# Attention over all heads as one sequence, and TensorE in source order from the first value unit on

## The chip, the cores and the metric

The kernel runs on one core of one Trainium2 chip. The metric is device microseconds (us) of one execution. The time of the kernel before is the median of three runs; a profile comes from one further execution, recorded by the hardware profiler.

## The reference, cut to what matters

One block of a hybrid model, sequence 512, width 2048, float32 throughout: a norm, one large input projection `w_in`, a state-space mixer (SSD) and an attention mixer side by side, the output projection `w_out`, and a gated feed-forward part.

```python
u = rmsnorm(h, attn_norm_w)
z, xbc, dt_raw, q, kc, vc, ks, vs, kw, vw, gate_raw = split(u @ w_in)
y_ssd = ssd_mixer(z, xbc, dt_raw, ...)        # ends: rmsnorm(y * silu(z), norm_w)
y_att = nsa_mixer(q, kc, vc, ks, vs, kw, vw, gate_raw, ...)
h = h + concatenate([y_ssd, y_att]) @ w_out
v = rmsnorm(h, ffn_norm_w)
h = h + (silu(v @ w_gate) * (v @ w_up)) @ w_down
out = rmsnorm(h, final_norm_w)

# nsa_mixer: 16 query heads of 64 in 4 groups; each group shares one key/value head
k_cmp = silu(flat(kc + pe_k) @ w1_k) @ w2_k   # 31 blocks of 32 tokens; v_cmp alike
o_cmp = softmax(q . k_cmp, masked) @ v_cmp
o_sel = softmax(q_rot . rope(ks) over the chosen blocks) @ vs    # 8 of 8 blocks
o_win = softmax(q_rot . rope(kw), window 512) @ vw
y_att = g0*o_cmp + g1*o_sel + g2*o_win        # g = sigmoid(gate_raw)
```

With 512 tokens the choice takes all 8 blocks and the window spans the sequence, so `o_sel` and `o_win` are both full causal attention, each with its own keys and values. They are the two branches (`br` 0 and 1) below.

## The kernel before, in words

**Units.** Both projections are cut into units of 128 output columns: 41 input units (`w_in`), then 16 output units (`w_out`). `run_unit` loops over the contraction in steps of 128. The activations stand in SBUF as `u`, a high and a low part; weights arrive as `wraw` (256 KB loads on SyncE's (SP's) queue, a ring of four) and are split into `whi` (ScalarE, ACT) and `wlo` (VectorE, DVE). A step `k` issues three matmuls into a bank `ps_g`, and after them the scheduler of the source, `Sched`, ticks once:

```python
pe.matmul(p, hi_t[i][:, j, :], ah, start=(k == 0), stop=False)                  # L234
pe.matmul(p, hi_t[i][:, j, :], al, start=False, stop=False)                     # L235
pe.matmul(p, lo_t[i][:, j, :], ah, start=False, stop=(k == u.nk - 1))           # L236
sch.tick()
```

An input unit has 16 steps; the output units have 11, 11, thirteen times 12, and 8 (table `NS`), and the rest of `w_out` is added by the part behind them.

**Tasks.** Everything else is a generator task: `yield n` means that the task goes on n ticks later, and a task can wait for flags that others set. So the source interleaves the tasks' instructions with the units' matmuls; how closely is set by the yields. `run_until(flags)` ticks on the spot, without any unit matmul between, until the flags are there.

**Two orders.** The framework has a scheduler of its own that moves instructions on every engine against source order. Only within `tc.manual_schedule(engines=PE)` does TensorE (PE) keep the order of the source. Before the change that holds from the first output unit on (`units[NU:]`, NU = 41).

**Order of the input units.** Gates and time steps, the state-space inputs, the four that feed the compression, `z` tiles 0 to 3, then for each group g its remaining `z` tiles (g=1: two, g=2: one, g=3: one), values `VS`, keys `KS` and two query units `Q`. A z tile's evacuation multiplies `silu(z)` with the mixer's row tile, stores the product to DRAM (`gy`) and adds its square to `acc2` (square on ACT, sum on POOL); after tile 7 `rms_stats` makes the second norm's row `row2`.

**Compression.** `compress()` (L599 to L681) takes 16 blocks of `w1` weights, eight for keys, then eight for values. A block: a load `w1r` (GpSimd (POOL) queue, two buffers), its split into `w1h` (ACT) and `w1l` (DVE), the inputs `xh` and `xl`, then six matmuls into `ps_s` (L630 to L632). Then two tails, for keys and values: transposes (L642), `hf`, `hh`, `hl`, small matmuls with `w2` (L663 to L665 and L677 to L679), and out come `kch`, `kcl` and `vcmp`. `pre_att`, run ahead of the first value unit, calls `run_until("cmp", ...)`, so that in the source the whole compression ends ahead of that unit's matmuls.

**Attention.** It loops over the four groups. At a group's start it waits for the group's keys, values and both query units, then does the compressed softmax (`sc`), its transposes `cph`, `cpl`, and four pairs of copies into `vpad`. Then come 32 items (head, branch, block of 128 queries): a score (two matmuls with `kh`, `kl` and the rotated queries `rq` into a bank `ps_s`, L834 and L835; DVE's mask-and-minimum L838 empties the bank into `e`; ACT's exponential), three items later the transposes (L863 into `ps_t`, split into `pth` and `ptl`), and after four transposed items the value matmuls (L873, L874, L879 into `ps_v`). An item takes 1 tick plus `PACE[s % 4]` ticks, or `PACE_OUT` once the output units have begun. A query unit's evacuation makes the rotated queries (rope: four small DMAs `sw` on POOL's queue, POOL arithmetic), `uq` on POOL, and the compressed scores (L776, L777 into `ps_m`, 16 pairs of small matmuls a unit).

**The end of the input units.** `pre_ms`, ahead of the last input unit, starts `ms_in`: eight times a `gy` row tile is loaded, multiplied by `row2` on POOL (L134), and written, scaled, over the first half of `u` (high part ACT, low part DVE L972). `ma_in` does the same for attention rows that went to DRAM. The first output unit reads both.

**PSUM.** Besides two banks `ps_g` the tasks share `ps_s`, `ps_t`, `ps_m` and `ps_v`.

Of the kernel before, what the change touches and what calls it, by code (L numbers as in the profile page):

```python
# [29 lines left out]
PACE = [2,2,2,3]  # L30
PACE_OUT = [1,2,1,2]
LAG = 3
# [83 lines left out]
def body(ctx, tc, xT, w_in, w_out, w_gate, w_up, w_down, w1k, w1v, cols, rows, kst, out):  # L116
# [35 lines left out]
    def ps_t():  # L152
        return ps("t", 2)
# [394 lines left out]
    def ev_z(t):  # L548
        def ev(p):
# [209 lines left out]
    def ev_q(g, j):  # L759
        def ev(p):  # L760
# [6 lines left out]
            yield 2  # L767
# [19 lines left out]
    def attention():  # L787
# [6 lines left out]
        for g in range(4):  # L794
            yield from sch.wait(("k", g), ("v", g), ("q", g, 0), ("q", g, 1))
            kh, kl = R["k", g]
            v = R["v", g]

            sc = R["sc", g]
            sm = ap.tile([128, 3, 4, 4], F32, tag="sm", name="sm", bufs=1)  # L800
            dve.tensor_reduce(sm[:, 0], sc, AX.X, ALU.max)
            dve.tensor_scalar(sm[:, 0], sm[:, 0], -1e20, None, op0=ALU.max)
            dve.tensor_tensor(sc.rearrange("p i h k -> p (i h) k"), sc.rearrange("p i h k -> p (i h) k"),
                              sm[:, 0].rearrange("p i h -> p (i h)")[:, :, None].to_broadcast([128, 16, 32]),
                              ALU.subtract)
            act.activation(sc, sc, AF.Exp, scale=0.125)
            for h in range(4):
                a_hi(vpad[32 * h:32 * h + 32, h, 0:64], vcmp[:, g, :])
                lo(dve, vpad[32 * h:32 * h + 32, h, 64:128], vcmp[:, g, :], vpad[32 * h:32 * h + 32, h, 0:64])
# [4 lines left out]
            mul(dve, sc.rearrange("p i h k -> p (i h) k"), sc.rearrange("p i h k -> p (i h) k"),  # L814
                sm[:, 2].rearrange("p i h -> p (i h)")[:, :, None].to_broadcast([128, 16, 32]))
            yield 6
            p = ps_t()
# [7 lines left out]
            yield 2  # L825

            items = [(h, br, i) for h in range(4) for br in range(2) for i in range(4)]
            pt, pr, po = {}, {}, {}

            def score(h, br, i):  # L830
                L = 128 * (i + 1)
                q = R["rq", g, h // 2][:, h % 2, i * 128:(i + 1) * 128]
                p = ps_s()
                pe.matmul(p[:, 0:L], q, kh[:, br, 0:L], start=True, stop=False)  # L834
                pe.matmul(p[:, 0:L], q, kl[:, br, 0:L], start=False, stop=True)  # L835
                e = ap.tile([128, 512], F32, tag="e", name="e", bufs=EB)
                m = ap.tile([128, 4], F32, tag="em", name="em", bufs=EB + 1)
                dve.tensor_tensor_reduce(e[:, 0:L], p[:, 0:L], kcs(K_AM + 512 - L, L), -0.125, 3e38,  # L838
                                         ALU.add, ALU.min, m[:, 0:1])
                act.activation(e[:, 0:L], e[:, 0:L], AF.Exp, scale=-1.0, bias=m[:, 0:1], accum_out=m[:, 1:2])  # L840
                pr[h, br, i] = (e, m)

            def norm(h, br, i):
                L = 128 * (i + 1)
                e, m = pr[h, br, i]
                gc = (4 * g + h) * 3 + 1 + br
                dve.reciprocal(m[:, 2:3], m[:, 1:2])
                if br:
                    dve.tensor_scalar(e[:, 0:L], e[:, 0:L], m[:, 2:3], gat[:, i, gc:gc + 1],
                                       op0=ALU.mult, op1=ALU.mult)  # L850
                else:
                    mul(dve, m[:, 3:4], m[:, 2:3], gat[:, i, gc:gc + 1])
                    a_hi(e[:, 0:L], e[:, 0:L], scale=m[:, 3:4])

            def trans(h, br, i):
                e, m = pr.pop((h, br, i))
                if i == 0:
                    pt[h, br] = (ap.tile([128, 13, 128], F32R, tag="pth", name="pth", bufs=2),
                                 ap.tile([128, 13, 128], F32R, tag="ptl", name="ptl", bufs=2))
                th, tl = pt[h, br]  # L860
                p = ps_t()
                for kb in range(i + 1):
                    pe.transpose(p[:, kb * 128:(kb + 1) * 128], e[:, kb * 128:(kb + 1) * 128], ident)  # L863
                s = p[:, 0:128 * (i + 1)].rearrange("p (a b) -> p a b", b=128)
                d = slice(i, 3 * i + i + 1, 3)
                a_hi(th[:, d, :], s)
                lo(dve, tl[:, d, :], s, th[:, d, :])

            def pvmm(h, br):
                th, tl = pt.pop((h, br))  # L870
                if br == 0:
                    o = po[h] = ps_v()
                    pe.matmul(o, vpad[:, h, :], ch, start=True, stop=False)  # L873
                    pe.matmul(o, vpad[:, h, :], cl, start=False, stop=False)  # L874
                o = po[h]
                for kb in range(4):
                    for t in (th, tl):
                        rhs = t[:, 4 * kb:3 * kb + 4, :].rearrange("p a b -> p (a b)")
                        pe.matmul(o[:, kb * 128:512], v[:, kb, br, :], rhs, start=False,  # L879
                                  stop=(br == 1 and kb == 3 and t is tl))  # L880
                if br == 1:
                    if h % 2 == 0:
                        R["at"] = ap.tile([128, 512], F32, tag="at", name="at", bufs=1)
                    at = R["at"]
                    a, b = (0, 64) if h % 2 == 0 else (64, 0)
                    fo = ap.tile([128, 512], F32, tag="fo", name="fo", bufs=1)
                    act.activation(fo[a:a + 64, :], o[b:b + 64, :], AF.Copy)
                    add(dve, at[a:a + 64, :], o[a:a + 64, :], fo[a:a + 64, :])
                    if h % 2:
                        k = 2 * g + h // 2  # L890
                        if "ma" in P2:
                            h_, l_ = P2["ma"][k]
                            a_hi(h_, at)
                            lo(dve, l_, at, h_)
                        else:
                            nc.gpsimd.dma_start(at_d[k], at)
                            P2["at"] = k
                        sch.flags.add(("at", k))

            n = len(items)  # L900
            for s in range(n + LAG + 1):
                if s < n:
                    score(*items[s])
                    if items[s][1:] == (1, 3):
                        sch.flags.add(("h", g, items[s][0]))
                yield 1
                if 0 <= s - LAG < n:
                    trans(*items[s - LAG])
                if s < n:
                    norm(*items[s])  # L910
                yield P2.get("pace", PACE)[s % len(PACE)]
                if 0 <= s - LAG - 1 < n and items[s - LAG - 1][2] == 3:
                    pvmm(*items[s - LAG - 1][:2])
            sch.flags.add(("a", g))
# [895 lines left out]
    for n, u in enumerate(units):  # L1810
# [98 lines left out]
```

## Time and profile before

| | us |
|---|---|
| median of 3 runs | 2240.73 |
| lowest, highest | 2238.62, 2245.78 |
| profiled execution | 2243.56 |
| its span on the engines | 2241.8 |

| engine | busy us | share of the span |
|---|---|---|
| PE matmuls | 2167.7 | 97% |
| DVE | 1794.5 | 80% |
| ACT | 1196.4 | 53% |
| POOL | 432.3 | 19% |

The mean granted TensorE clock is 0.986. In rows of the profile an operation is written out<-in with the program's tile names, L834 is a line of the kernel, and an arrow "<-DVE em L838" names what released the instruction and ended its wait. A row of stretches reads: window, its length, then busy time and instructions of PE, of PE's weight loads, DVE, ACT, POOL; then granted clock, share of DMA, and GB/s. The first matmul L234 of a unit starts at 7.0 us, the last at 822.6; and the rest is the feed-forward part, which the change does not touch.

### The profile page before, as it was taken

How to read it: one execution, taken by the hardware profiler on the slowest of the kernel's cores; microseconds unless marked ns; L12 is line 12 of the kernel's file. 1: busy time of each engine (PE TensorE's matmuls, PEld its weight loads, DVE VectorE, ACT ScalarE, POOL GpSimd, SP SyncE). 2: the span in 40 equal slices, each digit the busy share in tenths (PEclk: the TensorE clock that was granted, in tenths of full speed). 3: DMA queues.
4: the chain of work that ended last, by engine and by line, in shares of the span. 5: the costliest groups of instructions: out<-in, count | busy, mean ns of one | idle time of the engine just before them, and what ended most of it. 6: DMA issues, size and time to landing. Idle time of an engine off the chain costs nothing. (4 is left out here: it accounts for less than half of the span.)

```text
span 2241.8 us, 34995 instructions
## 1 busy us (share of the span) xinstructions
PE 2167.7 (97%) x12892; PEld 1908.6 (85%) x12892; DVE 1794.5 (80%) x2821; ACT 1196.4 (53%) x1991; POOL 432.3 (19%) x439
## 2 busy tenths in 40 slices
PE   7999999999999999999999999999999899999996
PEld 5888888888878887888888888888888889999996
DVE  7699766778886648988888888888887878888886
ACT  4564446666666657555555555555555333333453
POOL 2011225234331126000100000000000122221232
PEclk9999999999979999999999999999999999999998
DMA  5222343222334367788888788887878869686974
GB/s 179 90 71 76 120 151 100 76 83 69 97 88 116 104 189 226 223 222 251 227 228 235 219 249 231 239 235 214 249 218 268 315 197 307 191 283 183 298 184 135
DMA packets 170492, 416.66 MB, mean 186 GB/s; under 512 B 16800, under 2 KB 23984, under 8 KB 170320
## 3 DMA queue, kind: packets, MB, share of 16 engines
q1 hardware_dynamic: 98912, 246.73, 33.0%
q0 software_dynamic: 28112, 80.65, 18.4%
q10 hardware_dynamic: 43296, 87.04, 10.8%
q8 instruction: 101, 1.65, 0.3%
q14 instruction: 71, 0.58, 0.1%
HBM read 353.54 MB, written 57.15 MB: 183 GB/s over the span
## 5 line engine op out<-in xcount | busy, mean ns | idle before, releaser
L125 ACT ACTIVATE R<-Z 128x1024 fp32r<-128x1024 f32 (+4 forms) x458 | 415.5, 922 | 438.7 <-DVE Z L137 322.7
L128 DVE TENSOR_TENSOR R<-Z,R 128x1024 fp32r<-128x1024 f32 (+4 forms) x367 | 386.1, 1061 | 35.9 <-ACT R L125 21.1
L234 PE MATMUL ps_g<-u,whi 128*128 128x512 f32 x778 | 316.0, 406 | 0.0
L236 PE MATMUL ps_g<-u,wlo 128*128 128x512 f32 x778 | 307.7, 395 | 0.0
L235 PE MATMUL ps_g<-u,whi 128*128 128x512 f32 x778 | 306.3, 394 | 0.0
L1180 PE MATMUL ps_s<-u,R 128*128 128x512 f32 (+1 forms) x1160 | 252.9, 348 | 7.1 <-ACT A L1390 6.8
L128 DVE TENSOR_TENSOR wlo<-wraw,whi 128x512 fp32r<-128x512 f32 x211 | 159.5, 757 | 80.8 <-ACT whi L125 77.5
L1180 PEld LDWEIGHTS ps_s<-u,R 128*128 128x128 f32 x1160 | 187.7, 188 | 38.7 <-ACT A L1390 12.2
L125 ACT ACTIVATE whi<-wraw 128x512 fp32r<-128x512 f32 x211 | 131.9, 625 | 144.8 <-PE ps_g L235 98.6
L236 PEld LDWEIGHTS ps_g<-u,wlo 128*128 128x128 f32 x778 | 146.6, 188 | 30.6
L234 PEld LDWEIGHTS ps_g<-u,whi 128*128 128x128 f32 x778 | 147.0, 189 | 24.9 <-issue 0.2
L235 PEld LDWEIGHTS ps_g<-u,whi 128*128 128x128 f32 x778 | 147.1, 189 | 23.8
L1180 PE MATMUL ps_t<-u,R 128*128 128x512 f32 (+1 forms) x600 | 131.4, 347 | 0.0
L1180 PE MATMUL ps_g<-u,R 128*128 128x512 f32 x584 | 131.3, 349 | 0.0
L1180 PE MATMUL ps_s<-T,R 128*128 128x512 f32 (+1 forms) x560 | 125.7, 349 | 1.3 <-DVE R L128 1.3
L1180 PE MATMUL ps_g<-T,R 128*128 128x512 f32 (+1 forms) x584 | 125.7, 346 | 0.0
L1180 PE MATMUL ps_s<-V,R 128*128 128x512 f32 (+1 forms) x568 | 123.1, 347 | 0.0
L125 ACT ACTIVATE R<-A 128x1024 fp32r<-128x1024 f32 (+3 forms) x76 | 71.0, 934 | 86.3 <-DVE A L137 62.2
L137 DVE TENSOR_TENSOR Z<-Z 128x1024 f32<-128x1024 f32 (+5 forms) x96 | 106.1, 1105 | 8.8 <-POOL E L137 4.2
L137 DVE TENSOR_TENSOR A<-ps_g,A 128x512 f32<-128x512 f32 (+1 forms) x110 | 71.1, 653 | 51.5 <-PE ps_g L1180 38.6
L128 DVE TENSOR_TENSOR E<-Z,R 128x1024 fp32r<-128x1024 f32 (+1 forms) x91 | 109.9, 1208 | 1.5 <-ACT R L125 1.0
L1180 PEld LDWEIGHTS ps_t<-u,R 128*128 128x128 f32 x600 | 98.0, 188 | 14.1
(487 smaller groups left out, 5621.4 us busy)
## 6 DMA issues: line engine op xcount, KB each, us to landing
Z<-in_w_up SPq DMA_DIRECT2D x94, 512.0 KB, 5.3
Z<-in_w_gate SPq DMA_DIRECT2D x94, 512.0 KB, 6.4
wraw<-in_w_in SPq DMA_DIRECT2D x164, 256.0 KB, 2.5
g_d<-A ACTq DMA_DIRECT2D x22, 1792.0 KB, 15.0
Z<-in_w_up POOLq DMA_DIRECT2D x37, 512.0 KB, 8.9
Z<-in_w_gate POOLq DMA_DIRECT2D x37, 512.0 KB, 7.0
Z<-in_w_down SPq DMA_DIRECT2D x59, 320.0 KB, 5.7
Z<-in_w_down SPq DMA_DIRECT2D x41, 384.0 KB, 4.1
```

What stands on the lines that cost most here:

```text
L125: act.activation(dst, src, AF.Copy, scale=scale)
L128: eng.tensor_tensor(dst, src, f(hi), ALU.subtract)
L137: eng.tensor_tensor(o, a, b, ALU.add)
L234: pe.matmul(p, hi_t[i][:, j, :], ah, start=(k == 0), stop=False)
L235: pe.matmul(p, hi_t[i][:, j, :], al, start=False, stop=False)
L236: pe.matmul(p, lo_t[i][:, j, :], ah, start=False, stop=(k == u.nk - 1))
L1180: pe.matmul(o, w, x, start=start, stop=(k == n - 1 and o is q), skip_group_check=not fresh[0])
```

## The change

It has six parts, all in the attention part and its surroundings; the arithmetic of each operation stays.

1. `manual_schedule` on PE begins at the first value unit (`n_att`) instead of the first output unit: 20 input units more.
2. The four groups' items become one sequence of 128, with the three-item lag running on across groups. The waits are finer: keys and first query unit at a group's first item, the second query unit at head 2, values and compressed softmax (`cc`) ahead of the first value matmuls.
3. The compressed softmax is a task `compressed(g)` of its own, started for group g+1 at head 2 of group g, and spread by more yields; its `vpad` copies stand behind its transposes.
4. One pace, `[2,2,2,2,2,2,2,3]`, for all items; `PACE_OUT` goes.
5. Longer yields: ahead of the value transposes 2 to 6, ahead of the compressed scores 2 to 10, 12 ahead of the second norm, whose `gap` goes from 4 to 8.
6. In group 3 the first query unit goes ahead of the value and key units.

```diff
-PACE = [2,2,2,3]
-PACE_OUT = [1,2,1,2]
+PACE = [2,2,2,2,2,2,2,3]
...
             if t == 7:
+                yield 12
                 P2["row2"] = sp.tile([128, 512], F32, tag="yz", name="row2", bufs=1)
-                sch.add(rms_stats(acc2, 1024, P2["row2"], "r2"))
+                sch.add(rms_stats(acc2, 1024, P2["row2"], "r2", gap=8))
...
             mul(dve, t, p, rrow)          # ev_vs
-            yield 2
+            yield 6
...
             uq = q_stack(ap, "uq", 1, t, pool)   # ev_q
-            yield 2
+            yield 10
...
-        for g in range(4):
-            yield from sch.wait(("k", g), ("v", g), ("q", g, 0), ("q", g, 1))
...
+        def compressed(g):
+            yield from sch.wait(("q", g, 0), ("q", g, 1))
...
+            mul(dve, rows, rows, wide(2))
             yield 6
+            if g:
+                yield from sch.wait(("pv", g - 1, 3, 0))
             p = ps_t()
...
+            R["cc", g] = (ch, cl)
+            sch.flags.add(("cc", g))
...
+        items = [(g, h, br, i) for g in range(4) for h in range(4) for br in range(2) for i in range(4)]
+        n = len(items)
+        sch.add(compressed(0))
+        for s in range(n + LAG + 1):
+            if s < n:
+                g, h, br, i = items[s]
+                if (h, br, i) == (0, 0, 0):
+                    yield from sch.wait(("k", g), ("q", g, 0))
+                if (h, br, i) == (2, 0, 0):
+                    yield from sch.wait(("q", g, 1))
+                if (h, br, i) == (2, 0, 2) and g < 3:
+                    sch.add(compressed(g + 1))
+                score(*items[s])
...
+            yield 1
+            if 0 <= s - LAG < n:
+                trans(*items[s - LAG])
+            if s < n:
+                norm(*items[s])
+            yield PACE[s % len(PACE)]
+            if 0 <= s - LAG - 1 < n and items[s - LAG - 1][3] == 3:
+                g, h, br, _ = items[s - LAG - 1]
+                if (h, br) == (0, 0):
+                    yield from sch.wait(("v", g), ("cc", g))
+                pvmm(g, h, br)
+                sch.flags.add(("pv", g, h, br))
...
-        order += [U_Z[t] for t in z] + [U_VS[g], U_KS[g]] + U_Q[g]
+        vk, q = [U_VS[g], U_KS[g]], U_Q[g]
+        order += [U_Z[t] for t in z] + (vk + q if g < 3 else q[:1] + vk + q[1:])
...
     def pre_out():
-        P2["pace"] = PACE_OUT
...
+    n_att = order.index(U_VS[0])
-    for n, u in enumerate(units):
+    for n, u in enumerate(units[:n_att]):
...
-        if n == NU:
-            break
         run_unit(u)
     with tc.manual_schedule(engines={mybir.EngineType.PE}):
-        for u in units[NU:]:
+        for u in units[n_att:]:
             run_unit(u)
```

Lines of the new kernel are mostly one lower up to L577 (its unit matmuls are L233 to L235), the same in `compress`, and different in attention.

The order on PE is the same in both kernels up to the end of the input unit ahead of the first value unit. There, before the change, the framework's scheduler set the compression's matmuls (`ps_s<-w1h,xh`) between those of the first value unit (`ps_g_3160`):

```order
L234 MATMUL ps_g_3160<-u_91,whi_2950 128x512
L235 MATMUL ps_g_3160<-u_91,whi_2950 128x512
L630 MATMUL ps_s_2446<-w1h_2683,xh_2688 124x256
L236 MATMUL ps_g_3160<-u_91,wlo_2951 128x512
L234 MATMUL ps_g_3160<-u_91,whi_2950 128x512
L235 MATMUL ps_g_3160<-u_91,whi_2950 128x512
L236 MATMUL ps_g_3160<-u_91,wlo_2951 128x512
L631 MATMUL ps_s_2446<-w1l_2684,xh_2688 124x256
L632 MATMUL ps_s_2446<-w1h_2683,xl_2689 124x256
```

After the change the unit's matmuls begin only behind the compression. What follows the transposes of the last z tile (`ps_m`), which stood there before too, is:

```order
L558 MATMUL ps_m_3064<-ident_74,xt_641 128x128 x4
L630 MATMUL ps_s_2446<-w1h_2683,xh_2688 124x256
L631 MATMUL ps_s_2446<-w1l_2684,xh_2688 124x256
L632 MATMUL ps_s_2446<-w1h_2683,xl_2689 124x256
L630 MATMUL ps_s_2446<-w1h_2683,xh_2688 124x256
L631 MATMUL ps_s_2446<-w1l_2684,xh_2688 124x256
L632 MATMUL ps_s_2446<-w1h_2683,xl_2689 124x256
```

and so on for ten blocks and both tails, 92 rows with no `ps_g` among them, up to the last small matmuls of the value tail and the unit's first:

```order
L677 MATMUL ps_s_3125<-w2vh_3121,hh_3114 32x64
L678 MATMUL ps_s_3125<-w2vl_3122,hh_3114 32x64
L679 MATMUL ps_s_3125<-w2vh_3121,hl_3115 32x64
L233 MATMUL ps_g_3162<-u_91,whi_2950 128x512
L234 MATMUL ps_g_3162<-u_91,whi_2950 128x512
L235 MATMUL ps_g_3162<-u_91,wlo_2951 128x512
```

The order now alternates no longer: the unit's first matmul stands 92 rows later.

At the other end of the input units, on PE before the change, between the last input unit and the first output unit (`ps_g_6506`, some 40 rows further down), there stand scores, transposes, value matmuls and the last query unit's compressed scores, with no unit matmul between them:

```order
L834 MATMUL ps_s_6459<-kh_5097,rq_5293 128x512
L835 MATMUL ps_s_6459<-kl_5098,rq_5293 128x512
L873 MATMUL ps_v_6522<-cph_6185,vpad_3170 128x512
L874 MATMUL ps_v_6522<-cpl_6186,vpad_3170 128x512
L863 MATMUL ps_t_6404<-ident_74,e_6248 128x128 x3
L863 MATMUL ps_t_6433<-ident_74,e_6287 128x128 x4
L776 MATMUL ps_m_6304<-kch_85,uq_6269 128x32
L777 MATMUL ps_m_6304<-kcl_86,uq_6269 128x32
```

After the change, on PE at the same place, the first output unit's matmuls (`ps_g_6638`) stand between the score of item 79, counted from 0 (`ps_s_6654`), transposes, value matmuls and the score of item 80 (`ps_s_6706`, 25 rows after that of item 79):

```order
L234 MATMUL ps_g_6638<-u_91,whi_6467 128x512
L235 MATMUL ps_g_6638<-u_91,wlo_6468 128x512
L841 MATMUL ps_s_6654<-kh_5234,rq_5535 128x512
L842 MATMUL ps_s_6654<-kl_5235,rq_5535 128x512
L233 MATMUL ps_g_6638<-u_91,whi_6467 128x512
L234 MATMUL ps_g_6638<-u_91,whi_6467 128x512
L235 MATMUL ps_g_6638<-u_91,wlo_6468 128x512
L870 MATMUL ps_t_6669<-ident_74,e_6535 128x128
L233 MATMUL ps_g_6638<-u_91,whi_6467 128x512
L234 MATMUL ps_g_6638<-u_91,whi_6467 128x512
L235 MATMUL ps_g_6638<-u_91,wlo_6468 128x512
```

So tasks that stood alone there now alternate with unit matmuls. On DVE after the change, between emptying the banks of those two scores (items 79 and 80), there stand the scaled z rows over `u`, two splits of weights, rotated queries, splits of transposes and scalings of `e`:

```order
L996 SCALAR_TENSOR_TENSOR u_91<-gy_6506,colc_72,u_91 128x512
L127 TENSOR_TENSOR ptl_6668<-ps_t_6669,pth_6667 128x128
L854 RECIPROCAL em_6658<-em_6658 128x1
L856 TENSOR_SCALAR e_6603<-e_6603,em_6604,gat_79 128x384
L996 SCALAR_TENSOR_TENSOR u_91<-gy_6549,colc_72,u_91 128x512
L856 TENSOR_SCALAR e_6657<-e_6657,em_6658,gat_79 128x512
L127 TENSOR_TENSOR wlo_6684<-wraw_6515,whi_6683 128x512
L996 SCALAR_TENSOR_TENSOR u_91<-gy_6567,colc_72,u_91 128x512
L127 TENSOR_TENSOR rq_6789<-ro_6630,rq_6789 64x512 x2
L996 SCALAR_TENSOR_TENSOR u_91<-gy_6592,colc_72,u_91 128x512
L996 SCALAR_TENSOR_TENSOR u_91<-gy_6619,colc_72,u_91 128x512
L127 TENSOR_TENSOR vpad_3172<-vcmp_87,vpad_3172 32x64
```

More of the change, by code (lines that the diff above doesn't have):

```diff
@@ L825, in attention @@
             yield 2
[L827 to L905, printed above, removed]
-                yield 1
[L907 to L913, printed above, removed]
@@ L914, in attention, with score @@
-            sch.flags.add(("a", g))
+            for h in range(4):
+                a_hi(vpad[32 * h:32 * h + 32, h, 0:64], vcmp[:, g, :])
+                lo(dve, vpad[32 * h:32 * h + 32, h, 64:128], vcmp[:, g, :], vpad[32 * h:32 * h + 32, h, 0:64])
+                yield 1
+            yield 3
+            R["cc", g] = (ch, cl)
+            sch.flags.add(("cc", g))
+        pt, pr, po = {}, {}, {}
+        def score(g, h, br, i):
+            L = 128 * (i + 1)
+            q = R["rq", g, h // 2][:, h % 2, i * 128:(i + 1) * 128]
+            p = ps_s()
+            kh, kl = R["k", g]
+            pe.matmul(p[:, 0:L], q, kh[:, br, 0:L], start=True, stop=False)
+            pe.matmul(p[:, 0:L], q, kl[:, br, 0:L], start=False, stop=True)
+            e = ap.tile([128, 512], F32, tag="e", name="e", bufs=EB)
+            m = ap.tile([128, 4], F32, tag="em", name="em", bufs=EB + 1)
+            dve.tensor_tensor_reduce(e[:, 0:L], p[:, 0:L], kcs(K_AM + 512 - L, L), -0.125, 3e38,
+                                     ALU.add, ALU.min, m[:, 0:1])
+            act.activation(e[:, 0:L], e[:, 0:L], AF.Exp, scale=-1.0, bias=m[:, 0:1], accum_out=m[:, 1:2])
+            pr[g, h, br, i] = (e, m)
@@ new lines, in trans @@
+        def trans(g, h, br, i):
+            e, m = pr.pop((g, h, br, i))
+            if i == 0:
+                pt[g, h, br] = (ap.tile([128, 13, 128], F32R, tag="pth", name="pth", bufs=2),
+                             ap.tile([128, 13, 128], F32R, tag="ptl", name="ptl", bufs=2))
+            th, tl = pt[g, h, br]
+            p = ps_t()
+            for kb in range(i + 1):
+                pe.transpose(p[:, kb * 128:(kb + 1) * 128], e[:, kb * 128:(kb + 1) * 128], ident)
+            s = p[:, 0:128 * (i + 1)].rearrange("p (a b) -> p a b", b=128)
+            d = slice(i, 3 * i + i + 1, 3)
+            a_hi(th[:, d, :], s)
+            lo(dve, tl[:, d, :], s, th[:, d, :])
@@ new lines, in pvmm @@
+        def pvmm(g, h, br):
+            th, tl = pt.pop((g, h, br))
+            if br == 0:
+                ch, cl = R["cc", g]
+                o = po[h] = ps_v()
+                pe.matmul(o, vpad[:, h, :], ch, start=True, stop=False)
+                pe.matmul(o, vpad[:, h, :], cl, start=False, stop=False)
+            o = po[h]
+            v = R["v", g]
+            for kb in range(4):
+                for t in (th, tl):
+                    rhs = t[:, 4 * kb:3 * kb + 4, :].rearrange("p a b -> p (a b)")
+                    pe.matmul(o[:, kb * 128:512], v[:, kb, br, :], rhs, start=False,
+                              stop=(br == 1 and kb == 3 and t is tl))
+            if br == 1:
+                if h % 2 == 0:
+                    R["at"] = ap.tile([128, 512], F32, tag="at", name="at", bufs=1)
+                at = R["at"]
+                a, b = (0, 64) if h % 2 == 0 else (64, 0)
+                fo = ap.tile([128, 512], F32, tag="fo", name="fo", bufs=1)
+                act.activation(fo[a:a + 64, :], o[b:b + 64, :], AF.Copy)
+                add(dve, at[a:a + 64, :], o[a:a + 64, :], fo[a:a + 64, :])
+                if h % 2:
+                    k = 2 * g + h // 2
+                    if "ma" in P2:
+                        h_, l_ = P2["ma"][k]
+                        a_hi(h_, at)
+                        lo(dve, l_, at, h_)
+                    else:
+                        nc.gpsimd.dma_start(at_d[k], at)
+                        P2["at"] = k
+                    sch.flags.add(("at", k))
```

32 lines of the change are left out of this document (22 added, 10 removed).

## The prediction

> **What bounds the kernel now.** I read the page first, then the stretches by engine, then the waits and single instructions where a stretch is not full.
>
> ```profile
> PE 2167.7 (97%) x12892; PEld 1908.6 (85%) x12892; DVE 1794.5 (80%) x2821; ACT 1196.4 (53%) x1991; POOL 432.3 (19%) x439
> ```
>
> TensorE (PE) is busy 97% of the span, so a new order can gain only where PE is idle or runs on a lowered clock. The changed part lies between about 300 and 840 us. Stretches of it, with each engine's busy time, its instructions in brackets, and the granted clock after POOL:
>
> ```profile
> 300.00:326.00 26.00, 26.00 (x144) 22.52 (x143) 19.80 (x44) 13.63 (x32) 7.15 (x12) 1.00 0.53 167
> 326.00:334.00 8.00, 6.34 (x57) 5.26 (x56) 3.23 (x6) 2.91 (x8) 0.00 (x0) 1.00 0.31 98
> 334.00:500.00 166.00, 166.00 (x853) 141.42 (x852) 116.70 (x288) 104.50 (x229) 60.01 (x63) 1.00 0.26 84
> 500.00:580.00 80.00, 79.53 (x427) 66.94 (x425) 63.99 (x170) 53.38 (x124) 27.43 (x28) 1.00 0.23 75
> 612.00:632.00 20.00, 14.42 (x64) 12.59 (x63) 19.82 (x35) 12.34 (x28) 15.39 (x15) 0.64 0.30 92
> 632.00:652.00 20.00, 17.32 (x73) 13.73 (x74) 17.58 (x51) 13.15 (x31) 4.46 (x4) 0.76 0.29 81
> 675.00:840.00 165.00, 165.00 (x830) 137.83 (x829) 98.49 (x269) 98.00 (x226) 27.97 (x39) 1.00 0.48 136
> ```
>
> So the scheduler's PE order is already full from 334 to 500. The one large hole is 612 to 652: idle 5.58 + 2.68 = 8.26 us, and a clock of 0.64 and 0.76, which over 20 us each is worth 7.2 + 4.8 = 12.0 us. VectorE (DVE) is busy 19.82 of the first 20 us there. PE's longest waits in that hole:
>
> ```profile
> PE ps_s L834 <- DVE em L838: 3.2, 1, 3.2
> PE ps_v L879 <- ACT pth L125: 1.4, 1, 1.4
> PE ps_m L776 <- POOL uq L128: 1.2, 1, 1.2
> ```
>
> A score waits for DVE to empty a score bank. That is where the old source-order region begins: what was traced earlier and was not yet done stood alone ahead of it, with no unit's matmuls between. The other stretch that matters is 300 to 334, full but for 1.66 us after 326. There the compression's matmuls stand between those of the first value unit:
>
> ```profile
> 300.06 0.47 PE L234 MATMUL ps_g<-u,whi 128*128 128x512 f32 x1
> 300.37 0.39 PE L235 MATMUL ps_g<-u,whi 128*128 128x512 f32 x1
> 300.60 0.28 PE L630 MATMUL ps_s<-w1h,xh 128*124 128x256 f32 x1
> 300.71 0.39 PE L236 MATMUL ps_g<-u,wlo 128*128 128x512 f32 x1
> 300.94 0.39 PE L234 MATMUL ps_g<-u,whi 128*128 128x512 f32 x1
> ```
>
> PE reaches the first value unit at 300.06; a unit's matmul takes 0.23 us (300.71 to 300.94).
>
> **A: the compression stands alone (a loss).** Source order now begins at that unit, and `pre_att` runs `compress()` to its end ahead of it. So 10 of its 16 blocks of weights (60 matmuls) and both tails come first, with no unit matmul among them: PE's cover for these chains is gone. What one block needs:
>
> ```profile
> L125 ACT ACTIVATE w1h<-w1r x16: 614/617/635, 274.7 to 324.2; 128x512 fp32r<-128x512 f32 x16
> L128 DVE TENSOR_TENSOR w1l<-w1r,w1h x16: 679/693/1449, 276.9 to 324.9; 128x512 fp32r<-128x512 f32 x16
> DMA to landing us min/median/max: 3.0/3.4/5.0
> 299.57 0.69 DVE L128 TENSOR_TENSOR w1l<-w1r,w1h 128x512 fp32r<-128x512 f32 x1 [1.25 <-ACT w1h L125]
> 300.56 0.55 POOL L612 DMA_DIRECT2D w1r<-in_w1v  x1 [1.97 <-DVE w1l L128]
> ```
>
> With two buffers, a load is issued when `w1l` of two blocks earlier is done: 299.57 + 0.69 = 300.26, issued 300.56, so 0.30 between. A round of two blocks is then 3.4 + 0.62 + 0.69 + 0.30 = 5.0 us. The second of the value branch's eight loads goes out at 300.56, as before the change; the last (three rounds on) at 300.56 + 15.0 + 1.1 = 316.7. The 1.1 is an estimate for the last z tile's evacuation, square and accumulation, which stand in the ACT, DVE and POOL orders during the first round. It is split at 316.7 + 4.7 = 321.4. The rest:
>
> ```profile
> 328.86 0.28 PE L632 MATMUL ps_s<-w1h,xl 128*124 128x256 f32 x1
> 329.91 0.28 PE L632 MATMUL ps_s<-w1h,xl 128*124 128x256 f32 x1
> 330.67 0.43 PE L642 MATMUL ps_t<-ident,hd 124*128 124x124 f32 x2 [0.47 <-ACT hd L635]
> 332.53 0.22 PE L679 MATMUL ps_s<-w2vh,hl 128*32 128x64 f32 x1 [0.21 <-DVE hl L128]
> 333.23 0.20 PE L679 MATMUL ps_s<-w2vh,hl 128*32 128x64 f32 x1
> ```
>
> Nine steps from 328.86 to 329.91, so 0.117 us a matmul: six take 0.7, sixty 7.0. A tail takes 332.53 - 330.67 = 1.86 us to its third small matmul and 0.7 more for the rest; the two tails, now one after the other, with 0.3 between for the memset and `kch`: about 5.5. The unit starts at 321.4 + 0.7 + 5.5 = 327.6. Of the 27.5 us since 300.06 PE works 7.0 + 1.7 (tails) = 8.7, so 18.8 are idle. Then the clock. Windows around its falls:
>
> ```profile
> 614.40:617.80 3.40, 1.17 (x4) 0.59 (x4) 3.34 (x10) 2.62 (x9) 2.07 (x4) 1.00 0.68 197
> 617.80:634.80 17.00, 15.09 (x60) 13.48 (x59) 16.81 (x27) 9.45 (x21) 12.28 (x11) 0.50 0.21 69
> 641.70:645.10 3.40, 1.81 (x10) 1.31 (x10) 2.93 (x10) 3.06 (x7) 0.00 (x0) 1.00 0.24 77
> 645.10:651.90 6.80, 5.71 (x22) 4.64 (x22) 5.08 (x21) 5.83 (x16) 1.52 (x2) 0.50 0.39 77
> 331.10:334.50 3.40, 2.22 (x32) 1.98 (x33) 2.32 (x4) 1.89 (x6) 0.21 (x1) 1.00 0.48 152
> ```
>
> After 3.4 us with 1.17 or 1.81 us of PE work the clock halved, and stayed so in steps of 3.4; after 2.22 it did not. A block of 0.7 us of matmuls every 2.5 us is less than either, so the block runs at half: 0.7 + 1.7 longer, and 1.7 us lost in the 3.4 us window before it comes back. A = 18.8 + 2.4 + 1.7 = 22.9, less the 1.7 idle after 326 that was there: **+21.2**. Bounds: 3.0 us landings (-1.6) and no halving (-4.1) give 15.5; 5.0 us landings give +6.4, 27.6. I take the median landing. The Trainium skill weighs against the halving: "TensorE: Matmul & The Clock Gate", section "HAM oscillation — how this bites in real kernels", wants idle gaps above about 3.4 us for it. The block's gaps would be 1.8 us; by that rule A is 17.1 and the time 2248. The trace differs: the clock fell after a gap of 3.2 us and again after one of 1.4.
>
> **B: the hole at 612 to 652 goes.** 8.26 + 12.0, less 1.5 counted twice (idle inside half-clock time is 1.91 + 1.09, half of it): **-18.8**. The steps that stood alone there (scores, the last query unit's compressed scores) now have unit matmuls between them, and group 3's softmax comes later.
>
> **C: what is late next.** The scaled z rows (`ms_in`) must still overwrite `u` while the last input unit reads it, and the first output unit needs them at once. In the new order DVE's stretch from score 79 to score 80 holds five of these, two `rq`, two splits, two `ptl`, three scalings:
>
> ```profile
> L134 POOL TENSOR_TENSOR gy<-gy,row x8: 1275/1302/1754, 602.7 to 631.6; 128x512 f32<-128x512 f32 x8
> L972 DVE SCALAR_TENSOR_TENSOR u<-gy,colc,u x8: 730/746/1395, 606.8 to 636.4; 128x512 fp32r<-128x512 f32 x8
> DMA to landing us min/median/max: 2.4/2.6/3.3
> L128 DVE TENSOR_TENSOR ptl<-ps_t,pth 128x512 fp32r<-128x512 f32 x4 | 2.7, 683 | 0.1
> ```
>
> The third row is the landing of the `gy` loads. By 0.75 for each `u` and 0.68 for each other full tile (shorter ones in proportion) that is about 9 us; PE between the two scores has 12 unit matmuls (2.8), ten value matmuls (2.0) and 0.5 more, 5.3. DVE is short by 3.5, and by 2 in the item before: 5.5 idle, plus one half-clock window (1.7): **+7.2**. Bounds: 3, if three items between a score and its transposes absorb half; 18.8, if it goes as it went before.
>
> **D, E: the other edits.** The 0.47 idle between 500 and 580 goes: -0.5. Source order itself costs PE nothing after 675, where it already ruled (165.00 of 165), although the pace there was closer (1, 2, 1, 2 and one tick more, so 2.5 ticks an item) than the new 2.125 + 1 = 3.125 everywhere. With 132 steps that is 412 ticks of the 498 that the twenty input and sixteen output units have; the start takes some 60, so attention ends before the last unit and uncovers nothing. Against 3.25 ticks in the input units the new pace is a little closer there, and the per-group starts (a wait of 8 ticks for the softmax) are gone; DVE's 116.70 of 166 us leaves room for both.
>
> `yield 10` ahead of the compressed scores, `yield 6` ahead of the value transposes, `yield 12` and `gap=8` around the second norm are no instructions: they set a later place on PE, so that `uq` (POOL, on whose queue four swap DMAs of rope go first), `vt` and `rst` are ready when PE comes. In the old hole the place was too early (the 1.2 us wait for `uq` above). The price of being late is nothing, as unit matmuls stand in between, but for the first group: its first score follows the query evacuation by 10 ticks, 16 small matmuls and three ticks, and its rotated queries, behind the same POOL queue, are about as late: **+2** (0 to 6, as group changes are where DVE has least room). Group 3's first query unit ahead of its value and key units takes its rope work off POOL before `ms_in` comes: it is part of what lets C be below the old hole. The new waits for `v`, `cc` and `pv` hold back tracing, not an engine. The softmax (`compressed`) keeps its instructions; its four `vpad` pairs stand behind the transposes and beside unit matmuls: nothing.
>
> **Sum.** 21.2 - 18.8 + 7.2 - 0.5 + 2 = +11.1. The profiled execution took 2243.56 (span 2241.8, 1.8 around it), 2.8 above the median of the three runs; on the median, 2240.7 + 11.1 = **2252**.
>
> **Rivals.** (1) The output boundary stalls as before (C = 18.8): 2263. DVE's 19.82 of 20 us speaks for it; that attention now spreads evenly, and group 3's softmax has left, against. (2) No change that can be told (0.3%, 6.7 us): the clock stays up in the block and loads land in 3.0, A = 15.5: 2246; or C is 3: 2248, with slightly shorter loads inside 0.3%. The wider gaps before each halving speak for the first. (3) Faster: weights' ring is full during the block, SP issues nothing, and loads land as `gy`'s may; at 2.4 us with no handover a round is 3.7, so A falls by 3 x 1.3 + 1.1 + 4.1 to 12.1, with C and E at nothing 2233. It decides below a round of about 3.8; no `w1r` load landed under 3.0, which speaks against. That source order changes nothing is out: the order of PE shows it.
>
> **How the numbers follow.** Forecast with its own range 2247.5 to 2259: 0.46; rival 1: 0.16; rival 2: 0.29; rival 3: 0.09. Slower by over 0.3% is the first two, 0.62; within, 0.29; faster, 0.09. The range takes A's and C's bounds, less a tenth at each end: 2236 to 2267.
>
> **What would show it.** In the trace after: PE near 300 to 328 under half busy, waiting for DVE `w1l` and then `hl`, clock 0.5; the first value unit's first matmul near 327.6; from there to the output units a full PE at clock 1.00; a few us of waits for `u` at the first output unit. Wrong it is if PE's idle time there is below 12 us, if weight loads land sooner, or if the attention runs with waits in every item.

## The result, and the profile after

| | before | after |
|---|---|---|
| median, us | 2242.26 (4 runs) | 2263.91 (4 runs) |
| lowest to highest | 2238.62 to 2245.78 | 2262.92 to 2267.41 |
| span of the profiled execution | 2241.8 | 2263.0 |
| mean granted clock | 0.986 | 0.983 |

The ratio is 1.0099, interval 1.0079 to 1.0120. The change costs 21.7 us by the medians; the forecast had 11. The direction held, and 2263.91 lies in the outer range (2236 to 2267), but it lies outside the forecast's own (2247.5 to 2259): the size was about twice the forecast. The line of the engines on the page after, and the stretches that answer to those of before (columns as there: PE, its weight loads, DVE, ACT, POOL, then clock, share of DMA and GB/s):

```profile
PE 2175.8 (96%) x12892; PEld 1908.0 (84%) x12892; DVE 1796.3 (79%) x2821; ACT 1199.6 (53%) x1991; POOL 434.6 (19%) x439
```

```profile
300.00:330.00 30.00, 21.51 (x101) 16.01 (x99) 17.53 (x39) 11.96 (x29) 7.14 (x12) 0.61 0.33 104
330.00:342.00 12.00, 12.00 (x47) 9.75 (x46) 2.95 (x7) 3.81 (x9) 0.00 (x0) 0.84 0.13 45
...
500.00:632.00 132.00, 129.90 (x698) 109.42 (x697) 103.49 (x276) 87.22 (x208) 36.71 (x39) 1.00 0.21 73
632.00:649.00 17.00, 16.40 (x87) 13.53 (x86) 14.45 (x35) 13.72 (x30) 11.74 (x11) 1.00 0.42 143
649.00:672.00 23.00, 13.29 (x47) 9.03 (x47) 21.74 (x34) 12.20 (x27) 16.42 (x14) 0.70 0.30 96
672.00:845.00 173.00, 172.96 (x889) 145.02 (x888) 107.56 (x308) 102.57 (x244) 21.12 (x29) 1.00 0.43 120
```

There are two holes now: the compression (300 to 342) and still one where the output units begin (649 to 672). In the second DVE is busy 21.74 of 23 us. The three largest of PE's waits between 300 and 850 (us in all, times, longest):

```profile
PE ps_g L234 <- DVE u L996: 9.2, 4, 5.7
PE ps_s L631 <- DVE w1l L127: 3.3, 6, 2.2
PE ps_s L630 <- ACT w1h L124: 2.4, 4, 1.4
```

To set the terms side by side I use one measure for every kernel here: the time from one PE matmul's start to the next, beyond the median for a matmul of that size in the kernel before, summed over a stretch. It holds idle time and lowered clock together. The stretches are the 56 us from the start of the unit ahead of the first value unit; from there to 2 us before the last input unit; and from there to 20 us after the second output unit's start.

| | ratio to before (interval) | compression | attention | output boundary |
|---|---|---|---|---|
| before | 1 | 2.1 | 0.7 | 19.6 |
| after | 1.0099 (1.0079 to 1.0120) | 22.1 | 6.2 | 15.0 |
| e1 | 1.0016 (1.0001 to 1.0031) | 3.9 | 6.7 | 16.6 |
| e2 | 1.0055 (1.0028 to 1.0081) | 21.1 | 3.5 | 13.8 |
| e3 | 1.0089 (1.0063 to 1.0114) | 21.5 | 6.2 | 15.5 |
| e4 | 0.9986 (0.9970 to 1.0002) | 3.7 | 0.2 | 17.0 |
| e5 | 1.0071 (1.0055 to 1.0088) | 21.3 | 6.4 | 15.6 |
| e6 | 1.0009 (0.9994 to 1.0024) | 4.0 | 9.5 | 15.1 |
| e7 | 1.0009 (0.9998 to 1.0019) | 2.2 | 0.7 | 16.8 |
| e8 | 1.0068 (1.0051 to 1.0085) | 5.6 | 6.9 | 18.6 |
| e9 | 1.0030 (1.0018 to 1.0043) | 6.7 | 5.8 | 17.1 |
| e10 | 1.0015 (1.0002 to 1.0027) | 5.6 | 5.8 | 12.6 |
| e11 | 0.9990 (0.9980 to 1.0000) | 5.3 | 6.7 | 7.3 |
| e12 | 0.9953 (0.9938 to 0.9968) | 2.2 | 1.7 | 6.9 |
| e13 | 0.9950 (0.9939 to 0.9962) | 3.7 | 1.7 | 7.5 |

For the change the differences are +20.0, +5.5 and -4.6, together 20.9 of the 21.2 us by which the span grew. Each row is one profiled execution. e1, e6 and e8 treat the attention alike and show 6.7, 9.5 and 6.9, so a difference of under 3 us between two rows tells nothing by itself. (The expectations below call the last hole of the changed kernel 16.8 or about 17: that counts it from 600 us.)

### The profile page after: what moved, and what is told of

Same layout as the page of the kernel before. It is cut to its first block, busy times and chain, and to the rows that moved or that the text cites. A ratio compares the mean times of both kernels' runs of the same rounds, so it can differ in the third digit from the quotient of the medians.

```text
span 2263.0 us, 34938 instructions
## 1 busy us (share of the span) xinstructions
PE 2175.8 (96%) x12892; PEld 1908.0 (84%) x12892; DVE 1796.3 (79%) x2821; ACT 1199.6 (53%) x1991; POOL 434.6 (19%) x439
## 5 line engine op out<-in xcount | busy, mean ns | idle before, releaser
L233 PE MATMUL ps_g<-u,whi 128*128 128x512 f32 x778 | 322.7, 415 | 0.0
L234 PE MATMUL ps_g<-u,whi 128*128 128x512 f32 x778 | 307.8, 396 | 9.2 <-DVE u L996 9.2
L235 PE MATMUL ps_g<-u,wlo 128*128 128x512 f32 x778 | 308.1, 396 | 0.0
L235 PEld LDWEIGHTS ps_g<-u,wlo 128*128 128x128 f32 x778 | 147.4, 189 | 32.0
L233 PEld LDWEIGHTS ps_g<-u,whi 128*128 128x128 f32 x778 | 147.8, 190 | 24.0
```

## The experiments

**e1: the compression out of the source-order region.**

```diff
+    units[n_att].pre()
+    units[n_att].pre = None
     with tc.manual_schedule(engines={mybir.EngineType.PE}):
         for u in units[n_att:]:
```

> Only what runs ahead of the first value unit (with the end of the compression) is traced before source order begins; all else as in the changed kernel. Theory A (the compression stands alone because it is traced inside the source-order region; in the changed kernel's trace PE loses 22.1 us there against 2.2 before): its matmuls go between the unit's again, first value unit at about 301 us, time 2244 (2241 to 2248). Rival: the weight loads of the compression bound that stretch whatever stands beside it, and the loss only moves: 2258 or more.

Ratio 1.0016, against 1.0099 with the block. The first value unit starts at 301.2, and its stretch reads

```profile
300.00:330.00 30.00, 27.40 (x174) 23.25 (x173) 20.96 (x45) 15.31 (x36) 7.28 (x12) 1.00 0.47 149
```

The clock is 1.00 where it was 0.61, and 18.2 of the 20.0 us are back. The median, 2249.15, is a little above the 2241 to 2248 that theory A gave, but `before` had 2244.45 on that chip; the rival's 2258 is out. Theory A is shown: the loss was made by tracing the end of the compression inside the region. The output boundary did not move (16.6), so that loss has another cause.

**e2: the value unit last in group 3.**

```diff
-        order += [U_Z[t] for t in z] + (vk + q if g < 3 else q[:1] + vk + q[1:])
+        order += [U_Z[t] for t in z] + (vk + q if g < 3 else vk[1:] + q + vk[:1])
```

> Group 3's units in the order keys, two query units, values, so that the last input unit brings no rope work to POOL (the last query unit's uq and rope take POOL 6.2 us in the hole at 650 to 669 of the changed kernel). Theory C1 (DVE's SBUF-to-SBUF instructions stand still while POOL works, and DVE's order then sets the z rows): the hole shrinks from 16.8 to about 8 to 12, time 2256 to 2260. Theory C2 (DVE is late by its own instructions alone): the value unit's evacuation has as many DVE instructions as a query unit's, time 2262 to 2266.

1.0055; the median 2259.39 and the span 2259.2 lie where C1 put them, the hole (13.8) does not. DVE's slowing beside POOL (what its instructions took beyond the median of the same shape with POOL silent) fell from 7.8 us to 2.1, so less rope work in the hole does free DVE, and yet the hole stays. That something else holds it as well is what the next runs try.

**e3: the row product on DVE.**

```diff
-            mul(pool, t, t, P2["row2"])
+            mul(dve, t, t, P2["row2"])
```

> The eight products of gy with the second norm's row go from POOL to DVE (POOL 8 x 1.3 to 1.8 us less, DVE 8 x 0.68 us more). Theory C1 (DVE stands still while POOL works): DVE loses about 4 of its 7 us of slowing and gains 3.4 us of work inside the hole; 2260 to 2264. Theory C2 (DVE's own instructions alone): the hole grows by 3 to 5: 2267 to 2270. Theory C3 (the z rows are late because POOL's queue is): the product no longer waits for rope work, hole at 3 to 7: 2250 to 2255.

Hole 15.5. C3, POOL's queue alone, has fallen; the interval does not tell C1 from C2. The trace shows why nothing was won: what DVE saves in slowing (3.5 us are left of 7.8) it now works, and it is full while PE starves.

```profile
645.00:655.00 10.00, 7.31 (x29) 5.74 (x28) 9.61 (x21) 9.20 (x22) 2.71 (x5) 0.83 0.44 147
655.00:665.00 10.00, 1.61 (x5) 0.80 (x4) 10.00 (x17) 4.04 (x8) 8.54 (x5) 0.77 0.25 76
```

**e4: source order from the first output unit, all else as changed** (`units[NU:]` again).

> All edits of the change but the start of source order, which is again the first output unit. Theory A: no loss at the compression; the scheduler's order then packs the input units as it did before, and the hole before the output units is back at 16 to 20 us: 2240 to 2246. Rival (one sequence and its pace alone empty the backlog at the boundary): hole below 8, 2228 to 2235. Rival (source order was needed for the new paces): waits in many items, over 2250.

0.9986, hole 17.0, attention 0.2. So the new paces, yields and the single sequence cost nothing in the scheduler's order, and they do not empty the boundary either: it stalls the same in either order.

**e5, e6, e7: the z rows land in place.** The changed kernel's z rows share a ring of four buffers (tag `raw`) with the weights. A load of `gy` goes out when DVE has read the tile before it in the ring: at 656.70, after `wlo` at 655.11 + 1.56; at 662.73, after the z row at 660.95 + 1.75 (the rows of SP and DVE stand below). The edit, alone, with e1's, and on the kernel before:

```diff
-            t = wp.tile([128, 512], F32, tag="raw", name="gy", bufs=4)
-            nc.sync.dma_start(t, gy_d[k])
-            mul(pool, t, t, P2["row2"])
+            nc.sync.dma_start(f(l_), gy_d[k])
+            t = wp.tile([128, 512], F32, tag="raw", name="gy", bufs=4)
+            mul(pool, t, f(l_), P2["row2"])
```

> The gy loads land in the low row of u that they will replace, not in a buffer of the ring of four that they share with the weights (POOL then writes the product into a ring buffer). Theory R (ring: in the changed kernel a gy load goes out only when DVE's u of two or three rows earlier frees a buffer, for instance 656.7 after 655.11 + 1.56, 662.73 after 660.95 + 1.75): the eight loads go out within the last input unit, the hole shrinks from about 17 us to 4 to 9, time 2253 to 2258. Theory C2 (DVE is short in that stretch whatever feeds it): hole within 3 us of what it was, 2261 to 2267. Rival against both: the weight loads queue behind the eight on SP and come late, hole over 18.

> The edits of e1 and e5 together. Theory R with theory A: hole 4 to 9 and compression at 4, so about 10 below e1 on the same chip: ratio to before 0.995 to 0.998. Theory C2: as e1, ratio about 1.0015.

> The kernel before with the edit of e5 alone. Theory R: the old hole of 19.6 us was the ring's too, so it falls to 6 to 12, ratio to before 0.994 to 0.997. Theory of the prediction (what stood alone ahead of source order made it): unchanged, ratio 0.999 to 1.001.

Ratios 1.0071, 1.0009, 1.0009; holes 15.6, 15.1, 16.8. Theory R alone has fallen in all three. In e6 the hole, with columns as above, is

```profile
630.00:655.00 25.00, 14.53 (x55) 10.61 (x53) 22.99 (x37) 16.05 (x35) 19.57 (x16) 0.73 0.20 64
```

POOL, rope and z rows together, is now busy 19.57 of 25 us and DVE 22.99, of which 6.9 are slowing. The loads come early, and DVE is late all the same.

**e8: slower items at the boundary** (e1, and a pace of 5 until the eighth z row).

> The edit of e1, and items take 1 + 5 ticks instead of 3.125 from the last input unit's start until the eighth z row is set, so that DVE has some 40% less attention work per unit matmul there. Theory C2: DVE's shortage goes, hole 16.6 to 5 to 9, ratio to before 0.996 to 0.999. Theory R: rows come by the ring's round trip, of which only DVE's waiting falls: hole 12 to 16, ratio 1.000 to 1.002; if the items then end after the last output unit, more.

1.0068, hole 18.6: a miss for both theories. PE's waits there:

```profile
PE ps_g L233 <- ACT u L124: 6.5, 3, 3.3
PE ps_g L234 <- DVE u L996: 5.2, 4, 3.5
PE ps_g L1207 <- DVE A L136: 2.7, 1, 2.7
```

PE still stands in front of the z rows. In the hole (629 to 656) DVE is now busy 21.54 of 27 us, no longer full, and POOL 21.21: DVE's attention work is not what held it. The third wait is behind the output units, where most of the miss in time lies: of the 12.7 us by which e8's span exceeds e1's, 9.7 come after the last step of the last output unit. That the items now end too late for what follows fits it, but was not tried by itself.

**e9, e10, e11: POOL in source order, then the last rope work behind the z rows, then both with the rows in place.** All three stand on e1. POOL keeps source order too: in the program built with the late rope and PE alone in source order, which was not run, POOL's order has the last key unit's rope ahead of five of the eight z rows again. The edit of e9 (the first two lines) and the late start of e10, shown for the last query unit (the last key unit the same, with 28):

```diff
-    with tc.manual_schedule(engines={mybir.EngineType.PE}):
+    with tc.manual_schedule(engines={mybir.EngineType.PE, mybir.EngineType.Pool}):
...
+            if (g, j) == (3, 1):
+                sch.add(late(22, ap, t))      # yield 22, then the same steps
+            else:
+                yield from query(ap, t)
```

> The edit of e1, and POOL keeps source order too from the first value unit on, so that seven of the eight z-row products stand in a row behind the last key unit's rope and ahead of the last query unit's. Theory D (DVE is short at the boundary: in e1 16.5 us of work and 7.6 us of standing still beside POOL in a hole of 24): POOL's work in that stretch is the same, only its order differs, so the hole stays at 13 to 17, ratio to before 1.000 to 1.003. Theory Q (the z rows wait for POOL's queue): hole below 8, ratio 0.996 to 0.998.

> As e9, and the rope work of group 3's last key and query units starts 28 and 22 ticks later, behind the eight z rows (some 12 us of POOL and 3.4 us of DVE work leave the hole). Theory D: DVE's demand there falls by 3.4 us and its standing still from 7.6 to about 3; hole 16.6 to 7 to 10, ratio to before 0.997 to 0.999. Theory R (ring of four): hole 13 to 16, ratio 1.000 to 1.002.

> The edits of e10 and e5 together. Theory D alone: as e10, within 2 us. Theories D and R together (each limit hides the other, so that e5 alone gained little): hole 3 to 6, ratio to before 0.994 to 0.997.

Ratios 1.0030, 1.0015, 0.9990; holes 17.1, 12.6, 7.3. In e9 DVE's slowing falls to 2.8 us and the hole stays: theory Q has fallen, and D alone does not explain it either. e10's hole lies between what theories D and R expected, its ratio where R did. e11 tells most: against e1, the rows in place alone (e6) gave 1.5 us of hole, the late rope alone (e10) 4.0, both 9.3 (16.6 to 7.3). By the ratios the same three are 1.6, 0.2 and 5.8 us; the intervals of e11 and e10 do not meet, those of e11 and e6 just do. It is more than D alone could give and less than was expected of both (hole 3 to 6, ratio 0.994 to 0.997), so something is left. The stretches of e10 and of e11:

```profile
631.00:655.00 24.00, 18.20 (x78) 13.94 (x77) 18.82 (x43) 15.69 (x37) 7.71 (x8) 0.86 0.38 120
```

```profile
628.00:652.00 24.00, 20.68 (x93) 16.26 (x92) 21.37 (x48) 17.26 (x41) 6.90 (x7) 0.86 0.28 96
```

In e10 DVE is no longer full (18.82 of 24): the z rows now wait for their loads (in five of eight cases the landing of a load is what lets the product on POOL start). In e11 it gets through 48 instructions in the 24 us, where the changed kernel's hole has 34 in 23.

**e12, e13: the same mending, with source order from four input units ahead of the output units** (`units[NU - 4:]`); e13 also slows the items there to a pace of 3.

> Late rope and rows in place as in e11, but source order (PE and POOL) begins only four input units ahead of the output units; the compression and most of the attention stand in the scheduler's order, as in e4. If the terms add up (compression 3.7 us lost as in e4, attention about 1, hole 7.3 as in e11, against 2.1, 0.7 and 19.6 before): 10 to 12 us below the kernel before, ratio 0.994 to 0.997. If the scheduler's order leaves a backlog that now stands alone at the new start: 0.998 to 1.002.

> As e12, and items take 4 ticks instead of 3.125 from the start of the last input unit until the eighth z row is set. Theory D (the rest of the hole is still DVE's load): hole 3 to 6, ratio 0.001 to 0.002 below e12. Rival (the z rows' chain of load, POOL, ACT and DVE bounds it): hole as in e12 within 1 us.

e12 has a ratio of 0.9953, median 2232.73: it is 0.5% below the kernel before, clear of the interval, and the terms add up (-11.6 us by the table, span 2231.6 against 2241.8). The compression is back under cover, and the clock is up again at the boundary (0.92 against 0.70):

```profile
300.00:330.00 30.00, 30.00 (x165) 25.90 (x164) 20.98 (x45) 15.21 (x33) 7.17 (x12) 1.00 0.49 158
...
623.00:645.00 22.00, 17.98 (x83) 14.11 (x82) 19.39 (x43) 15.70 (x37) 7.90 (x8) 0.92 0.24 78
```

e13 came out as e12 (0.9950, hole 7.5), against theory D and as its rival, the z rows' own chain, expected. What holds the last 7 us was not tried further and stays open.

## Why the prediction was wrong, step by step

**A, the compression: right in cause and size, wrong in one of its signs.** Forecast +21.2, measured +20.0, and e1 took 18.2 of them away with two lines. The last split of weights starts at 321.4, as forecast; then

```profile
L127 DVE TENSOR_TENSOR w1l<-w1r,w1h x9: 678/693/694, 299.7 to 321.4; 128x512 fp32r<-128x512 f32 x9
329.83 0.24 PE L679 MATMUL ps_s<-w2vh,hl 128*32 128x64 f32 x1
329.89 0.77 PE L233 MATMUL ps_g<-u,whi 128*128 128x512 f32 x1
```

the unit comes at 329.9 instead of 327.6, as the tails ran at half clock (the sum had 2.4 us for that). The clock did fall, although no wait of PE in the block was longer than 2.2 us: that decides for A's halved clock.

```profile
303.20:306.60 3.40, 1.54 (x7) 1.01 (x7) 3.40 (x6) 2.02 (x5) 2.37 (x3) 1.00 0.82 259
306.60:333.90 27.30, 21.60 (x85) 16.09 (x86) 11.89 (x32) 9.96 (x26) 4.22 (x8) 0.50 0.20 64
```

The Trainium skill, "TensorE: Matmul & The Clock Gate", section "HAM oscillation — how this bites in real kernels", which wants gaps above about 3.4 us, differs from the measurement here, and the 17.1 worked out from it was too low.

One sign that the prediction set for being wrong did come: PE idle below 12 us there. PE was busy 21.51 of the 30 us and idle 8.5. The 18.8 us of idle time counted the block's 8.7 us of matmuls at full clock; at half clock they step by about 0.21 us in place of 0.117. The chain of loads and splits still set the time (its last split came as forecast), so the same loss showed as slow matmuls where the prediction looked for idle time.

**B, the old hole: its waits went, its time mostly did not.** The forecast took off 18.8 us because work stood alone at the old start of source order. The waits did go: none of the three that the prediction lists for that hole comes back in the changed kernel's hole, where PE waits for `u` instead (9.2 us). e4, with source order from the first output unit again, waits for `u` too (9.8 us) and loses 17.0. So most of what B took off came back in C, and the two together measured 15.0 - 19.6 = -4.6, where the prediction had -18.8 + 7.2 = -11.6. DVE is full in both holes (19.82 of 20 us before, 21.74 of 23 after), but that one cause makes both is not shown: the waits differ, e7 kept the old ones (2.8 for the score bank, 2.0 for `uq`) and a hole of 16.8, and no run took the rope work out of the kernel before. Rival 1 said 2263 for this case and came nearest, with a chance of 0.16, and in part by luck: it had 18.8 for C and 1.5 for D and E, which measured 15.0 and 5.5.

**C, the output boundary: this is the step that failed.** The prediction put 9 us on DVE between emptying scores 79 and 80, and from that 5.5 us of idle PE and one window at half clock: C = 7.2. DVE took 654.50 to 670.77, 16.3 us, for the instructions that the order showed. PE was idle 9.7 us between 649 and 672, the clock stayed at half for four windows, and C measured 15.0:

```profile
654.80:668.40 13.60, 6.25 (x13) 4.04 (x14) 13.30 (x17) 4.87 (x8) 11.28 (x8) 0.50 0.29 92
```

From the stretch on DVE:

```profile
654.50 0.68 DVE L845 CUSTOM_DVE_ANT_0 e<-ps_s,kc 128x512 f32<-128x512 f32 x1
...
655.11 1.56 DVE L127 TENSOR_TENSOR wlo<-wraw,whi 128x512 fp32r<-128x512 f32 x1
656.60 1.35 DVE L856 TENSOR_SCALAR e<-e,em,gat 128x256 f32<-128x256 f32 x1
657.87 0.68 DVE L127 TENSOR_TENSOR ptl<-ps_t,pth 128x512 fp32r<-128x512 f32 x1
...
658.54 1.14 DVE L996 SCALAR_TENSOR_TENSOR u<-gy,colc,u 128x512 fp32r<-128x512 f32 x1
...
660.95 1.75 DVE L996 SCALAR_TENSOR_TENSOR u<-gy,colc,u 128x512 fp32r<-128x512 f32 x1
662.63 1.50 DVE L856 TENSOR_SCALAR e<-e,em,gat 128x512 f32<-128x512 f32 x1
664.05 0.68 DVE L127 TENSOR_TENSOR wlo<-wraw,whi 128x512 fp32r<-128x512 f32 x1
664.65 0.74 DVE L996 SCALAR_TENSOR_TENSOR u<-gy,colc,u 128x512 fp32r<-128x512 f32 x1
...
670.77 0.29 DVE L845 CUSTOM_DVE_ANT_0 e<-ps_s,kc 128x128 f32<-128x128 f32 x1
```

POOL at the same time (a line with two instructions has their sum), SP's loads, and PE behind them:

```profile
654.86 1.27 POOL L133 TENSOR_TENSOR gy<-gy,row 128x512 f32<-128x512 f32 x1 [1.19 <-DMA gy<-gy_d]
656.21 2.93 POOL L127 TENSOR_TENSOR uq<-qt,uq 64x512 fp32r<-64x512 f32 x2
659.21 1.60 POOL L133 TENSOR_TENSOR ro<-sw,kc 128x512 f32<-128x512 f32 x1
660.77 1.39 POOL L133 TENSOR_TENSOR gy<-gy,row 128x512 f32<-128x512 f32 x1
662.12 1.73 POOL L136 TENSOR_TENSOR ro<-ro,ro 128x512 f32<-128x512 f32 x1
665.56 1.69 POOL L133 TENSOR_TENSOR gy<-gy,row 128x512 f32<-128x512 f32 x1 [1.72 <-DMA gy<-gy_d]
```

```profile
656.70 0.32 SPq L993 DMA_DIRECT2D gy<-gy_d  x1
662.73 0.32 SPq L993 DMA_DIRECT2D gy<-gy_d  x1
```

```profile
659.73 0.79 PE L234 MATMUL ps_g<-u,whi 128*128 128x512 f32 x1 [5.67 <-DVE u L996]
662.76 0.79 PE L234 MATMUL ps_g<-u,whi 128*128 128x512 f32 x1 [1.38 <-DVE u L996]
```

Two things are to be seen. First, DVE's instructions were priced at their undisturbed durations (0.75 and 0.68). Grouped by shape, in the hole (649 to 672) and then in the calm stretch from 690 to 840:

```profile
L996 DVE SCALAR_TENSOR_TENSOR u<-gy,colc,u 128x512 fp32r<-128x512 f32 x6 | 7.0, 1169 | 0.5 <-ACT u L124 0.5
L127 DVE TENSOR_TENSOR wlo<-wraw,whi 128x512 fp32r<-128x512 f32 x2 | 2.2, 1121 | 0.0
L856 DVE TENSOR_SCALAR e<-e,em,gat 128x512 f32<-128x512 f32 x1 | 1.5, 1498 | 0.0
L127 DVE TENSOR_TENSOR ptl<-ps_t,pth 128x512 fp32r<-128x512 f32 x1 | 0.7, 678 | 0.0
```

```profile
L127 DVE TENSOR_TENSOR wlo<-wraw,whi 128x512 fp32r<-128x512 f32 x37 | 25.5, 690 | 15.2 <-ACT whi L124 12.9 <-PE ps_t L870 1.4 <-PE ps_v L882 0.8
L127 DVE TENSOR_TENSOR ptl<-ps_t,pth 128x512 fp32r<-128x512 f32 x12 | 8.3, 688 | 0.6
L856 DVE TENSOR_SCALAR e<-e,em,gat 128x512 f32<-128x512 f32 x6 | 3.3, 547 | 0.2
```

The scaling of `e`, which reads and writes SBUF, takes 1498 ns in the hole and 547 outside; the split of `ptl`, which reads PSUM, takes 678 and 688. Each slowed instruction in the stretch above runs beside a POOL instruction. From 663.85 to 665.56 POOL is silent, and there the same split and z row take 0.68 and 0.74 in place of 1.56 and 1.75. From 649 to 672 DVE's rows sum to 23.7 us where the same shapes without POOL beside them take 15.9: 7.8 us of slowing. The 6.8 of it between scores 79 and 80 are most of the 7.3 by which the 9 us were too low. The prediction's own rows held the hint, in a maximum of 1395 beside a median of 746 for these very z rows. The Trainium skill, "SBUF — State Buffer", section "SBUF: two separate sides", says that a GpSimd (POOL) instruction and a DVE instruction with two SBUF inputs or in a two-port mode take one pair of ports in turn, and that whichever starts first has it for its whole instruction; these rows agree, with 1.56 against 0.68 for the split of weights and 678 ns against 688 for `ptl`, which has one input from PSUM.

Second, the supply of z rows was not counted: the next load goes out only when DVE has freed a buffer of the weights' ring. Late DVE makes late loads, and late loads make late z rows (POOL waits 1.19 and 1.72 us for them above). So freeing DVE leaves the loads (e10), early loads leave DVE slowed (e6), and only e11, with both, takes more than half the hole. That the two limits need each other rests on e11 against e6 and e10. That the slowing is POOL's is seen in the durations, and it is smaller where POOL has less to do in the hole (e2, e3, e10: 2.1, 3.5 and 1.9 us), but no run silenced POOL alone.

The claim that group 3's new order takes rope work off POOL ahead of the z rows was wrong too: the key unit moved to second-last brings its own rope and `kl` (on POOL 1.49 for one `kl` at 648.51) in place of the first query unit's.

```profile
648.51 1.49 POOL L127 TENSOR_TENSOR kl<-ro,kh 64x512 fp32r<-64x512 f32 x1
```

**D and E, the rest of attention: the size is at the upper bound.** Forecast -0.5 and +2 (0 to 6), measured +5.5. (The 498 ticks that the prediction gives the units are 506 by the table `NS`; nothing hangs on it.) e4, with every edit but the order, has 0.2 there and e1 6.7, so the cost is source order's: it leaves PE waiting for `cpl` (1.6 us once) and for `uq` (0.9), and the clock fell once behind the latter (at 375, below), where the scheduler's order kept PE full. The late place set by `yield 10` did not cover `uq` in the first group.

**The sum.** The forecast had 21.2 - 11.6 + 1.5 = 11.1; measured 20.0 - 4.6 + 5.5 = 20.9. Of the 9.8 us missing, 7.0 are B and C and 4.0 are D and E, less 1.2 in A.

## What to carry to other kernels

A source-order region takes cover away from whatever is traced inside it before its own filler begins: trace a serial block ahead of the region, or start the region later. Where one stretch has a full DVE and a busy POOL, price DVE's SBUF-to-SBUF instructions at what they take beside POOL (here up to 1.75 us in place of 0.75), and look which buffers feed the chain: a hole that no single remedy moves may be held by two limits at once, and a kernel with both taken away can show it. A hole that stays at a boundary when the order changes is a reason to look at the data handed over there.

## What the runs showed of the hardware that was not expected

The slowing seems to go both ways: in e3, with a busier DVE, one pair of POOL's `uq` splits took 5.55 us, against 2.93 in the changed kernel; the median of all sixteen is 1.30 us each in both.

```profile
655.27 5.55 POOL L127 TENSOR_TENSOR uq<-qt,uq 64x512 fp32r<-64x512 f32 x2
```

The clock also fell after a window in which PE still worked most of the time, where the prediction had seen 2.22 us of 3.4 pass without a fall: after 2.49 us of work in small matmuls it stood at 0.51.

```profile
371.40:374.80 3.40, 2.49 (x20) 2.32 (x19) 0.45 (x2) 0.00 (x0) 3.24 (x3) 1.00 0.30 104
374.80:378.20 3.40, 3.40 (x9) 2.66 (x9) 2.20 (x4) 2.44 (x4) 0.86 (x1) 0.51 0.00 0
```

So the share of work in such a window does not by itself say whether the clock falls.
